# Attention scores as three 64-row products per segment, with two heads in different rows of the array, and the gates' weights copied behind the first layer's operands

## The chip, the cores and the metric

The kernel runs on one core of a Trainium2 chip. It uses TensorE (PE in the profile; its weight loads are PEld), VectorE (DVE), ScalarE (ACT), GpSimd (POOL) and SyncE (SP, which here only issues DMAs). The metric is device time in microseconds (us), the median of the timed runs; less is better.

## The reference

The program is a decoder trunk of two layers on 512 rows of width 1024, in float32. The first mixes rows by gated linear attention, the second by stick-breaking attention over 16 heads of 64; behind each stand a layer norm, an MLP of width 4096 with a squared ReLU, and another layer norm. The change touches the first products of the first layer (a projection of x, of which the last 16 columns feed the forget gates) and the scores of the second layer's attention:

```
proj = x @ w_in
q, k, v, g, a1 = jnp.split(proj, [GLA_QK, 2 * GLA_QK, 2 * GLA_QK + GLA_V, 2 * GLA_QK + 2 * GLA_V], axis=-1)
log_a = jax.nn.log_sigmoid((a1 @ w_a2 + b_a).astype(jnp.float32)) / GATE_TAU
...
def stick_breaking_attention(q, k, v):
    # A[t,s] = sigmoid(z_ts) * prod_{s<j<t} (1 - sigmoid(z_tj)), z = q.k / sqrt(dh)
    for i in range(S // BLOCK_Q):                      # 4 blocks of 128 queries
        kv_len = (i + 1) * BLOCK_Q                     # causal: 128, 256, 384, 512 keys
        z = jnp.einsum('bqhd,bkhd->bhqk', q_blk, k_blk) * scale
        mask = s_idx[None, :] < t_idx[:, None]
        log_1m = jnp.where(mask, jax.nn.log_sigmoid(-z), 0.0)
        rev = lax.cumsum(log_1m, axis=3, reverse=True)
        log_w = jax.nn.log_sigmoid(z) + (rev - log_1m)
        w = jnp.where(mask, jnp.exp(log_w), 0.0)
        outs.append(jnp.einsum('bhqk,bkhd->bqhd', w, v_blk))
```

## The kernel before

**Products in three parts.** A float32 operand is split into a rounded part `hi` (type fp32r, an ACT copy) and the rest `lo` (a DVE subtract); `put` (L97 to L99) does both for a tile in PSUM or SBUF, `split_piece` (L70, L72) for a loaded piece of weights. A product is then three matmuls into one PSUM bank, hi x hi, hi x lo and lo x hi (`mm3`, lines L93, L94, L95). Rounded operands make a product of 512 columns take one pass. Where the operands stay float32, as in the transposes and in L826, it is the slower float32 form.

**PSUM.** There are eight banks of 512 float32 columns, given out in turn by `bank()`. A new tile waits until the last reader of the bank that it gets is done.

**Order.** Work is written in one order, and a scheduler places the instructions of each engine from it; instructions that are passed through `keep_in_program_order` stay in the written order among themselves.

**The start (L430 to L469).** x comes as eight tiles of 128 x 512 (L438, `h`), the first weights as eight pieces (L445, `raw`), alternating on SP's queue. For each step k from 0 to 7, four transposes turn the tile of x (L121), ACT and DVE copy the transposed tile out (`T`, L98 and L99) and split the weights (`hi`, `lo`, the same lines), and the products of the step before follow (L93 to L95, 96 of them in all). Transposes without a use (`warm`, L434 and L453) fill the first microseconds. In step 5 `gate_weights()` is called: it loads the gates' weights `wa_raw` and `a2` by eight small DMAs on SP (L408 to L423), copies `wa` on ACT and DVE (L411, L412), and splits `a2`. The first use of `wa` is the product of L468, behind the 96 products; `a2_hi` follows later.

**Attention (L755 to L880).** Eight pairs of heads, p = 0 to 7; a pair fills 128 partitions, one head in partitions 0 to 63 and the other in 64 to 127. Of a pair:
- `keys()` and `queries()` project 128 columns of keys or queries: 24 products of 512 columns (L93 to L95) into one bank. Out of it the tiles for the scores are made. They hold, for each head, hi and lo stacked over 128 rows: `kh` is the keys' hi in both halves of the rows (an ACT copy, L767, and a POOL copy into the other half, L770), `kl` the keys' lo in the head's own half beside zeros (DVE, L768), `qs` the queries' hi in the own half and lo in the other (ACT, L776; DVE, L777). Each works on the 64 partitions of one head, so each is done twice.
- `weights()` computes the scores in five tiles of one bank each (L790): for each of the segments of 512, 384 + 128, and 256 columns, two products of 128 rows, with `kh` and with `kl`. That is 16 products for the pair. Then DVE adds the mask (L794), ACT takes two sigmoids (`r`, L799; `w`, L800), DVE scans `r` (L802), and POOL (DVE for the last tile) multiplies (L803).
- `turn()` transposes the five tiles `w` (L812, four transposes for a tile) and copies them on ACT to `wt` (L817, eight copies for five tiles). It is a generator, and goes on by one tile each time that it is asked.
- `outputs()` multiplies `wt` with the values (L826): 16 products of 64 output rows, alternating between the heads, each head in its own half of the array's columns.

In the loop, turn p runs `keys` of pair p+2, then `queries` of pair p+2, during whose products the turning of pair p goes on (one tile behind each k of 4, 5, 6 and 7, by the table TAKE, and what is left at the end), then `weights` of pair p+1, then `outputs` of pair p. In p = 6 and 7, where no keys are left to project, the four row tiles of the output projection take their place.

Of the kernel before, what the change touches and what calls it, by code (L numbers as in the profile page):

```python
# [14 lines left out]
P = 128  # L15
S = 512
# [18 lines left out]
def yoco_kernel(ctx: ExitStack, tc: tile.TileContext, x, gla_w_in, gla_w_a2, gla_b_a, gla_norm_g,  # L35
# [369 lines left out]
    def gate_weights():  # L405

        wa_raw = gtp.tile([P, 8, RANK], F32, name="wa_raw")
        nc.sync.dma_start(out=wa_raw, in_=w_in[:, 2 * QK + 2 * D:].rearrange("(a p) c -> p a c", p=P))  # L408
        wa = gtp.tile([P, 8, P], F32R, name="wa")
        nc.gpsimd.memset(wa.bitcast(F32), 0.0)  # L410
        nc.scalar.activation(wa[:, :, 0:RANK], wa_raw, AF.Copy)  # L411
# [12 lines left out]
        return wa, a2_hi, a2_lo  # L424

# [10 lines left out]
    for u in range(2):  # L436
        for t in range(NT):
            nc.sync.dma_start(out=xs[t][:, 512 * u:512 * u + 512],  # L438
                              in_=x2[128 * t:128 * t + 128, 512 * u:512 * u + 512])
            if t % 2 == 0:  # L440
                trio = [wts.tile([P, 1024], dt, tag=tag, bufs=n, name=nm(tag))
                        for tag, dt, n in (("raw", F32, 3), ("hi", F32R, 6), ("lo", F32R, 6))]
            raw, hi, lo = (w[:, 512 * (t % 2):512 * (t % 2) + 512] for w in trio)
            k = 4 * u + t
            nc.sync.dma_start(out=raw, in_=w_in[128 * k:128 * k + 128, 2 * QK:2 * QK + 512])  # L445
            transpose_into(xT, u, t, xs[t][:, 512 * u:512 * u + 512], keep=tc.keep_in_program_order)
            put(hi, lo, raw, keep=tc.keep_in_program_order)
# [290 lines left out]
    kls = [sbp.tile([P, 2, S], F32R, name=f"kl{i}") for i in range(2)]  # L738
    for kl in kls:
        nc.gpsimd.memset(kl[DH:P, 0, :].bitcast(F32), 0.0)  # L740
        nc.gpsimd.memset(kl[0:DH, 1, :].bitcast(F32), 0.0)

    def chain():
        return sbp.tile([P, S], F32, tag="w", bufs=6, name=nm("w"))

# [10 lines left out]
    class Pair:  # L756


        def __init__(self, p):
            self.p = p  # L760

        def keys(self):
            ps = cols(h2T, piece_128(kv_w, P * self.p))
            self.kh = sbp.tile([P, 2, S], F32R, tag="kh", bufs=2, name=nm("kh"))
            self.kl = kls[self.p % 2]
            for a, (own, other) in enumerate(HALVES):
                nc.scalar.activation(self.kh[own, a, :], ps[own, :], AF.Copy)  # L767
                nc.vector.tensor_tensor(self.kl[own, a, :], ps[own, :], self.kh[own, a, :].bitcast(F32),  # L768
                                        op=ALU.subtract)
                nc.gpsimd.tensor_copy(out=self.kh[other, a, :], in_=self.kh[own, a, :])  # L770

        def queries(self, mid=None):
            ps = cols(h2T, piece_128(sb_w_q[0], P * self.p), mid)
            self.qs = sbp.tile([P, 2, S], F32R, tag="qs", bufs=2, name=nm("qs"))
            for a, (own, other) in enumerate(HALVES):
                nc.scalar.activation(self.qs[own, a, :], ps[own, :], AF.Copy, scale=DH ** -0.5)  # L776
                nc.vector.scalar_tensor_tensor(self.qs[other, a, :], ps[own, :], DH ** -0.5,  # L777
                                               self.qs[own, a, :].bitcast(F32), op0=ALU.mult, op1=ALU.subtract)

        def weights(self):  # L780

            self.ws = []
            for kind, segs in ((0, ((0, 3, 0),)), (1, ((0, 2, 0), (0, 0, 384))), (0, ((1, 3, 0),)),
                               (1, ((1, 2, 0), (1, 0, 384))), (2, ((0, 1, 0), (1, 1, 256)))):
                z = bank()
                for a, i, f in segs:
                    q = self.qs[:, a, P * i:P * i + P]
                    n = P * (i + 1)
                    for k, end in ((self.kh, False), (self.kl, True)):
                        nc.tensor.matmul(z[:, f:f + n], lhsT=q, rhs=k[:, a, 0:n], start=not end, stop=end)  # L790

                z4 = z.rearrange("p (b c) -> p b c", c=P)
                last = (z4[:, 3:4, :], z4[:, 2:4, :], z4[:, 1::2, :])[kind]
                nc.vector.tensor_tensor(last, last, low.unsqueeze(1).broadcast_to([P, last.shape[1], P]), op=ALU.add)  # L794
# [137 lines left out]
```

## Time and profile before

| | us |
|---|---|
| median of 3 runs (least, most) | 1143.9 (1143.76, 1144.88) |
| the profiled execution's own time | 1144.64 |
| its span | 1142.7 |
| PE busy | 1115.5 |
| DVE, ACT, POOL busy | 815.2, 554.2, 180.9 |

The span is the time between the first and the last recorded instruction; the profiled execution's own time is 1.9 us longer. In the rows below, L12 is line 12 of the kernel; x4 behind a shape counts instructions that are printed as one row; a bracket at the end of a row is the time that the engine had been idle, and what it waited for. A matmul's busy time holds its way through the array, which overlaps the next one's: the pace of the engine is read from start to start.

### The profile page before, as it was taken

Reading aid. Unit: us, or ns where it says so; the run is one execution under the profiler, and the core shown is the slowest. Engines: PE = TensorE matmul, PEld = TensorE weight load, DVE = VectorE, ACT = ScalarE, POOL = GpSimd, SP = SyncE. Lnnn points to the kernel's source line nnn. Section 1 sums busy time; section 2 is a strip of 40 time slices with the busy share of each in tenths; the row PEclk is TensorE's granted clock in tenths of the full one; section 3 lists DMA queues with packets and bytes.
Section 4 is the critical chain, followed back from the end, with each engine's and each line's share of the span. In section 5 each row is a group of like instructions: output and inputs, shape, how many; then the busy total and the mean of one; then the engine's idle time right before and its main releaser. Section 6 shows DMA issues by size and latency. Waiting matters only on the chain.

```text
span 1142.7 us, 14176 instructions
## 1 busy us (share of the span) xinstructions
PE 1115.5 (98%) x5435; PEld 927.9 (81%) x5435; DVE 815.2 (71%) x992; ACT 554.2 (48%) x823; POOL 180.9 (16%) x217
## 2 busy tenths in 40 slices
PE   7999999999999999999999999999999999999995
PEld 6888888898888888888788877787988888888884
DVE  2678738977757847839946878796767767567578
ACT  2554436553533534536635575654544435336262
POOL 1010123010000100121202435350100000001221
PEclk8999999999999999999999999999999999999998
DMA  7531299492670770886344121211864815706871
GB/s 214 148 111 56 81 267 204 132 295 109 180 207 21 201 203 19 216 189 129 94 128 129 56 75 37 74 38 37 241 202 115 240 51 150 227 28 185 193 120 74
DMA packets 104936, 156.47 MB, mean 137 GB/s; under 512 B 12258, under 2 KB 37218, under 8 KB 104868
## 3 DMA queue, kind: packets, MB, share of 16 engines
q1 hardware_dynamic: 86916, 120.96, 33.1%
q0 software_dynamic: 17952, 34.61, 17.6%
q8 instruction: 42, 0.69, 0.2%
q14 instruction: 26, 0.21, 0.1%
HBM read 153.45 MB, written 2.10 MB: 136 GB/s over the span
## 4 chain that ended last, share of the span: by engine, by line
PE 86%; DVE 8%; ACT 3%; issue 1%; DMA 1%; POOL 0%; SPq 0%; DVEq 0%; ACTq 0%; POOLq 0%
PE ps L336 26%; PE ps L93 18%; PE ps L94 18%; PE ps L95 18%; DVE lo L72 2%; PE ps L826 2%; PE ps L812 1%; ACT wt L817 1%; DVE T L99 1%; DVE h L168 1%; DVE bst L175 1%; ACT hi L70 1%; DVE r L802 1%; DVE h L194 1%; DMA h<-in_x_dram 1%
## 5 line engine op out<-in xcount | busy, mean ns | idle before, releaser
L336 PE MATMUL ps<-hi,T 128*128 128x512 f32 x1008 | 313.2, 390 | 0.0
L93 PE MATMUL ps<-T,hi 128*128 128x512 f32 (+1 forms) x768 | 288.3, 376 | 0.0
L94 PE MATMUL ps<-T,hi 128*128 128x512 f32 (+1 forms) x768 | 285.7, 372 | 0.9 <-DVE T L99 0.8
L95 PE MATMUL ps<-T,lo 128*128 128x512 f32 (+1 forms) x768 | 285.3, 372 | 0.0
L72 DVE TENSOR_TENSOR lo<-raw,hi 128x1024 fp32r<-128x1024 f32 x134 | 164.1, 1228 | 131.9 <-ACT hi L70 131.4
L70 ACT ACTIVATE hi<-raw 128x1024 fp32r<-128x1024 f32 x134 | 142.5, 1065 | 179.8 <-PE ps L336 62.1
L336 PEld LDWEIGHTS ps<-hi,T 128*128 128x128 f32 x1008 | 188.9, 188 | 40.1 <-DVE T L99 0.8
L336 PE MATMUL ps<-lo,T 128*128 128x512 f32 x504 | 196.3, 389 | 0.0
L72 DVE TENSOR_TENSOR lo<-B,hi 128x1024 fp32r<-128x1024 f32 x108 | 130.9, 1223 | 88.5 <-ACT hi L70 88.3
L70 ACT ACTIVATE hi<-B 128x1024 fp32r<-128x1024 f32 x108 | 114.3, 1059 | 150.3 <-PE ps L94 78.7
L95 PEld LDWEIGHTS ps<-T,lo 128*128 128x128 f32 x768 | 144.6, 188 | 25.3
L94 PEld LDWEIGHTS ps<-T,hi 128*128 128x128 f32 x768 | 144.8, 189 | 24.9 <-DVE T L99 1.3
L93 PEld LDWEIGHTS ps<-T,hi 128*128 128x128 f32 x768 | 144.5, 188 | 24.7 <-issue 0.9
L290 POOL DMA_DIRECT2D B<-in_mlp_w_down_dram x52 | 62.4, 1226 | 539.2 <-DMA B<-in_mlp_w_down_dram 464.8
L336 PEld LDWEIGHTS ps<-lo,T 128*128 128x128 f32 x504 | 94.6, 188 | 19.5
L93 PE MATMUL ps<-hi,T 128*128 128x512 f32 x256 | 103.0, 402 | 5.2 <-ACT T L98 5.2
L94 PE MATMUL ps<-lo,T 128*128 128x512 f32 x256 | 100.9, 394 | 0.8 <-DVE lo L72 0.8
L95 PE MATMUL ps<-hi,T 128*128 128x512 f32 x256 | 100.8, 394 | 0.0
L168 DVE TENSOR_TENSOR h<-h,ps 128x512 f32<-128x512 f32 x110 | 74.6, 682 | 5.2 <-PE ps L95 3.6
L803 POOL TENSOR_TENSOR w<-w,r 128x512 f32<-128x512 f32 x32 | 55.0, 1720 | 55.7 <-DVE r L802 38.4
L802 DVE TENSOR_TENSOR_SCAN r<-r,begin 128x512 f32<-128x512 f32 x40 | 61.1, 1559 | 0.2
L93 PEld LDWEIGHTS ps<-hi,T 128*128 128x128 f32 x256 | 48.5, 189 | 15.1 <-ACT T L98 5.4
(173 smaller groups left out, 1203.0 us busy)
## 6 DMA issues: line engine op xcount, KB each, us to landing
raw<-in_mlp_w_up_dram SPq DMA_DIRECT2D x64, 512.0 KB, 5.4
B<-in_mlp_w_down_dram SPq DMA_DIRECT2D x64, 512.0 KB, 5.8
B<-in_mlp_w_down_dram POOLq DMA_DIRECT2D x52, 512.0 KB, 7.9
raw<-in_gla_w_in_dram SPq DMA_DIRECT2D x20, 512.0 KB, 3.7
raw<-in_mlp_w_down_dram SPq DMA_DIRECT2D x16, 512.0 KB, 4.9
raw<-in_kv_w_dram SPq DMA_DIRECT2D x16, 512.0 KB, 3.7
B<-in_gla_w_o_dram POOLq DMA_DIRECT2D x14, 512.0 KB, 9.5
B<-in_gla_w_o_dram SPq DMA_DIRECT2D x8, 512.0 KB, 8.3
```

What stands on the lines that cost most here:

```text
L70: nc.scalar.activation(hi, raw, AF.Copy)
L72: nc.vector.tensor_tensor(lo, raw, hi.bitcast(F32), op=ALU.subtract)
L93: nc.tensor.matmul(ps, lhsT=a[0], rhs=b[0], start=first, stop=False)
L94: nc.tensor.matmul(ps, lhsT=a[0], rhs=b[1], start=False, stop=False)
L95: nc.tensor.matmul(ps, lhsT=a[1], rhs=b[0], start=False, stop=last)
L99: keep(nc.vector.tensor_tensor(lo, ps, hi.bitcast(F32), op=ALU.subtract))
L168: nc.vector.tensor_tensor(h, h, ps, op=op)
L290: nc.gpsimd.dma_start(out=b.rearrange("p (a b) -> p a b", a=2), in_=weights(k, h, j), accum_op=ALU.add)
L336: nc.tensor.matmul(banks[s], lhsT=a(k, s)[x], rhs=b[k][y], start=opens and (k, x, y) == (0, 0, 0), stop=closes and (k, x, y) == (3, 1, 0), ...
L802: nc.vector.tensor_tensor_scan(down, down, begins[kind][:, ::-1], 1.0, op0=ALU.mult, op1=ALU.max)
L803: (nc.vector if kind == 2 else nc.gpsimd).tensor_tensor(w, w, r[:, 1:S + 1], op=ALU.mult)
L826: nc.tensor.matmul(ops[HALVES[a][0], P * j:512], lhsT=vs[hd // 8][:, j, DH * (hd % 8):DH * (hd % 8) + DH], rhs=self.wt[a][:, 512 * j:512 * ...
```

## The change

Three parts.

1. The gates' weights: `gate_weights()` is called behind the loop of the first products instead of in its step 5, and both of its splits go through `put` in the written order.
2. The scores: the tiles of a pair are `kh`, `kl`, `qh`, `ql`, each with both heads over 128 partitions, so each is one instruction (two for the keys, two for the queries). POOL's copies and the zeros beside `kl` are gone. `scores()` makes three products of 64 rows for each segment and head (qh x kh, qh x kl, ql x kh), 24 for a pair, the two heads by turns, each from its own half of the rows and into its own bank: six banks instead of five. The last tile's two segments of 256 lie in two banks, so its mask and sigmoids are done in halves (six adds instead of five, twelve sigmoids instead of ten).
3. The turning: TAKE asks for two tiles behind k = 4, so all five are turned while the queries are projected; in p = 7 the four row tiles take 1, 1, 2 and 1 instead of 0, 1, 2 and 2.

```diff
@@ gate_weights()
-        nc.scalar.activation(wa[:, :, 0:RANK], wa_raw, AF.Copy)
-        nc.vector.tensor_tensor(wa[:, :, 32:32 + RANK], wa_raw, wa[:, :, 0:RANK].bitcast(F32), op=ALU.subtract)
+        put(wa[:, :, 0:RANK], wa[:, :, 32:32 + RANK], wa_raw, keep=tc.keep_in_program_order)
...
-        put(a2_hi, a2_lo, a2)
+        put(a2_hi, a2_lo, a2, keep=tc.keep_in_program_order)
@@ the loop of the first products
-            if k == 5:
-                wa, a2_hi, a2_lo = gate_weights()
...
+    wa, a2_hi, a2_lo = gate_weights()
     for j, kk in todo.pop():
         mm3(pss[j], xT.k(kk, 128 * j, 128), pcs[kk], kk == 0, kk == 7)
@@ class Pair
         def keys(self):
             ps = cols(h2T, piece_128(kv_w, P * self.p))
-            self.kh = sbp.tile([P, 2, S], F32R, tag="kh", bufs=2, name=nm("kh"))
-            self.kl = kls[self.p % 2]
-            for a, (own, other) in enumerate(HALVES):
-                nc.scalar.activation(self.kh[own, a, :], ps[own, :], AF.Copy)
-                nc.vector.tensor_tensor(self.kl[own, a, :], ps[own, :], self.kh[own, a, :].bitcast(F32),
-                                        op=ALU.subtract)
-                nc.gpsimd.tensor_copy(out=self.kh[other, a, :], in_=self.kh[own, a, :])
+            self.k = self.part("kh"), self.part("kl")
+            put(*self.k, ps)
...
-            for a, (own, other) in enumerate(HALVES):
-                nc.scalar.activation(self.qs[own, a, :], ps[own, :], AF.Copy, scale=DH ** -0.5)
-                nc.vector.scalar_tensor_tensor(self.qs[other, a, :], ps[own, :], DH ** -0.5,
-                                               self.qs[own, a, :].bitcast(F32), op0=ALU.mult, op1=ALU.subtract)
+            self.q = qh, ql = self.part("qh"), self.part("ql")
+            nc.scalar.activation(qh, ps, AF.Copy, scale=DH ** -0.5)
+            nc.vector.scalar_tensor_tensor(ql, ps, DH ** -0.5, qh.bitcast(F32), op0=ALU.mult, op1=ALU.subtract)
+
+        def scores(self):
+            zs = [bank() for _ in range(6)]
+            for i, b, f in ((3, 0, 0), (2, 2, 0), (0, 2, 384), (1, 4, 0)):
+                n = P * (i + 1)
+                for x, y in ((0, 0), (0, 1), (1, 0)):
+                    for a, (own, _) in enumerate(HALVES):
+                        at = slice(f + 256 * a * (i == 1), f + n + 256 * a * (i == 1))
+                        nc.tensor.matmul(zs[b + a][:, at], lhsT=self.q[x][own, P * i:P * i + P],
+                                         rhs=self.k[y][own, 0:n], start=(x + y == 0), stop=(x == 1),
+                                         skip_group_check=True)
+            return zs
@@ weights()
-                    for k, end in ((self.kh, False), (self.kl, True)):
-                        nc.tensor.matmul(z[:, f:f + n], lhsT=q, rhs=k[:, a, 0:n], start=not end, stop=end)
...
-                nc.scalar.activation(rb, z, AF.Sigmoid, scale=-1.0)
-                nc.scalar.activation(w, z, AF.Sigmoid)
+                for at, z in views:
+                    nc.scalar.activation(rb[:, at], z, AF.Sigmoid, scale=-1.0)
+                    nc.scalar.activation(w[:, at], z, AF.Sigmoid)
@@ the loop over the pairs
-    TAKE = {4: 1, 5: 1, 6: 1, 7: 1}
+    TAKE = {4: 2, 5: 1, 6: 1, 7: 1}
...
-            for _ in made:
-                pass
...
-                for _ in range((0, 1, 2, 2)[t]):
+                for _ in range(((0, 1, 2, 2), (1, 1, 2, 1))[n][t]):
                     next(made, None)
```

Two places of the new order. On ACT, at the start of the program, this is the difference (`T_101` are transposed tiles of x, `hi_121` the first split weights, `wa` the gates'):

```order
 L126 ACT_TABLE_LOAD
 L98 ACTIVATE T_101<-ps_124 128x4x128
 L98 ACTIVATE hi_121<-raw_120 128x512
-L411 ACTIVATE wa<-wa_raw 128x8x16
 L98 ACTIVATE T_101<-ps_145 128x4x128
 L98 ACTIVATE hi_121<-raw_120 128x512
```

The copy of `wa` stood ahead of the second transposed tile. It now stands behind the last operands of this stage:

```order
-L98 ACTIVATE T_103<-ps_303 128x4x128
-L98 ACTIVATE hi_280<-raw_279 128x512
+L98 ACTIVATE T_103<-ps_284 128x4x128
+L98 ACTIVATE hi_261<-raw_260 128x512
+L98 ACTIVATE wa<-wa_raw 128x8x16
+L98 ACTIVATE a_hi<-a_314 128x512
 L70 ACTIVATE hi_387<-raw_385 128x1024
```

(The first four rows are the last operands of the stage, the same ones under other buffer numbers.)

On SP the eight small loads of the gates' weights stood ahead of the last two tiles of x (`h_95`, `h_96`) and the last two pieces of weights; before:

```order
L445 DMA raw_211<-in_gla_w_in_dram 128x512
L408 DMA wa_raw<-in_gla_w_in_dram 128x8x16
L417 DMA a_262<-in_gla_w_a_dram 16x512
L418 DMA a_262<-in_gla_b_a_dram 1x512
...
L423 DMA normg<-in_gla_norm_g_dram 128x256
L438 DMA h_95<-in_x_dram 128x512
L445 DMA raw_279<-in_gla_w_in_dram 128x512
L438 DMA h_96<-in_x_dram 128x512
```

And now:

```order
L444 DMA raw_211<-in_gla_w_in_dram 128x512
L437 DMA h_95<-in_x_dram 128x512
L437 DMA h_96<-in_x_dram 128x512
L408 DMA wa_raw<-in_gla_w_in_dram 128x8x16
L416 DMA a_314<-in_gla_w_a_dram 16x512
...
L444 DMA raw_260<-in_gla_w_in_dram 128x512 x2
L417 DMA a_314<-in_gla_b_a_dram 1x512
```

Both tiles of x moved ahead of all the gates' loads; the last two pieces of weights stand behind five of those eight.

On PE, in the loop over the pairs, the end of a projection of queries (L93 to L95, with the transposes of the `w` tiles between), the scores, and the first of the outputs (`wt` is the turned weights, `T_4595` the values); before:

```order
L95 MATMUL ps_5345<-T_4179,lo_5343 128x512
L812 MATMUL ps_5403<-ident,w_5284 128x128 x4
L790 MATMUL ps_5410<-kh_5151,qs_5217 128x512
L790 MATMUL ps_5410<-kl_4589,qs_5217 128x512
L790 MATMUL ps_5421<-kh_5151,qs_5217 128x384
```

And now:

```order
L95 MATMUL ps_5348<-T_4179,lo_5346 128x512
L778 MATMUL ps_5412<-kh_5149,qh_5219 128x512
L778 MATMUL ps_5413<-kh_5149,qh_5219 128x512
L778 MATMUL ps_5412<-kl_5150,qh_5219 128x512
L778 MATMUL ps_5413<-kl_5150,qh_5219 128x512
L778 MATMUL ps_5412<-kh_5149,ql_5220 128x512
L778 MATMUL ps_5413<-kh_5149,ql_5220 128x512
```

The last transposes no longer stand between the projection and the scores, and the products of the two heads alternate between two banks. The two forms of L790 before have 128 rows of contraction each, the three forms of L778 have 64.

More of the change, by code (lines that the diff above doesn't have):

```diff
@@ L736, in yoco_kernel @@
     begins = (begin[:, 0:512], begin[:, 128:640], begin[:, 256:768])
[L738 to L741, printed above, removed]
     def chain():
@@ L760, in __init__, with part @@
             self.p = p
+        def part(self, tag):
+            return sbp.tile([P, S], F32R, tag=tag, bufs=2, name=nm(tag))
         def keys(self):
             ps = cols(h2T, piece_128(kv_w, P * self.p))
-            self.kh = sbp.tile([P, 2, S], F32R, tag="kh", bufs=2, name=nm("kh"))
-            self.kl = kls[self.p % 2]
-            for a, (own, other) in enumerate(HALVES):
-                nc.scalar.activation(self.kh[own, a, :], ps[own, :], AF.Copy)
-                nc.vector.tensor_tensor(self.kl[own, a, :], ps[own, :], self.kh[own, a, :].bitcast(F32),
-                                        op=ALU.subtract)
-                nc.gpsimd.tensor_copy(out=self.kh[other, a, :], in_=self.kh[own, a, :])
+            self.k = self.part("kh"), self.part("kl")
+            put(*self.k, ps)
@@ L772, in queries @@
         def queries(self, mid=None):
             ps = cols(h2T, piece_128(sb_w_q[0], P * self.p), mid)
-            self.qs = sbp.tile([P, 2, S], F32R, tag="qs", bufs=2, name=nm("qs"))
-            for a, (own, other) in enumerate(HALVES):
-                nc.scalar.activation(self.qs[own, a, :], ps[own, :], AF.Copy, scale=DH ** -0.5)
-                nc.vector.scalar_tensor_tensor(self.qs[other, a, :], ps[own, :], DH ** -0.5,
-                                               self.qs[own, a, :].bitcast(F32), op0=ALU.mult, op1=ALU.subtract)
+            self.q = qh, ql = self.part("qh"), self.part("ql")
@@ L780, in weights @@
         def weights(self):
             self.ws = []
[L783 to L788, printed above, removed]
-                    for k, end in ((self.kh, False), (self.kl, True)):
[L790 to L794, printed above, removed]
+            zs = self.scores()
@@ new lines, in weights @@
+            for kind, segs, banks in ((0, ((0, 3, 0),), (0,)), (0, ((1, 3, 0),), (1,)), (1, ((0, 2, 0), (0, 0, 384)), (2,)),
+                                      (1, ((1, 2, 0), (1, 0, 384)), (3,)), (2, ((0, 1, 0), (1, 1, 256)), (4, 5))):
+                n = S // len(banks)
+                views = [(slice(n * i, n * i + n), zs[b][:, n * i:n * i + n]) for i, b in enumerate(banks)]
+                for _, z in views:
+                    z4 = z.rearrange("p (b c) -> p b c", c=P)
+                    last = z4[:, (slice(3, 4), slice(2, 4), slice(1, 2))[kind], :]
+                    nc.vector.tensor_tensor(last, last, low.unsqueeze(1).broadcast_to([P, last.shape[1], P]),
+                                            op=ALU.add)
```

## The prediction

> **What bounds the kernel now.** I read the page's busy times first, then the chain that ended last:
>
> ```profile
> span 1142.7 us, 14176 instructions
> PE 1115.5 (98%) x5435; PEld 927.9 (81%) x5435; DVE 815.2 (71%) x992; ACT 554.2 (48%) x823; POOL 180.9 (16%) x217
> PE 86%; DVE 8%; ACT 3%; issue 1%; DMA 1%; POOL 0%; SPq 0%; DVEq 0%; ACTq 0%; POOLq 0%
> ```
>
> PE is the bound almost everywhere. A change can gain in only two ways: less streaming on PE, or less of PE's idle time, some 27 us in all. ACT, DVE and POOL count only where PE waits for them. So I read PE's timeline at both places of the change, start to start.
>
> **The start.** PE's, ACT's and SP's timelines, and two windows (columns: length; busy time of PE, PEld, DVE, ACT and POOL; granted clock; DMA share; GB/s):
>
> ```profile
> 5.94 0.60 PE L121 MATMUL ps<-ident,h 128*128 128x128 f32 x4
> 8.74 0.66 PE L121 MATMUL ps<-ident,h 128*128 128x128 f32 x4 [1.07 <-DMA h<-in_x_dram]
> 14.61 0.80 PE L93 MATMUL ps<-hi,T 128*128 128x512 f32 x1 [5.21 <-ACT T L98]
> 18.19 0.63 PE L95 MATMUL ps<-hi,T 128*128 128x512 f32 x1
> 18.62 0.76 PE L121 MATMUL ps<-ident,h 128*128 128x128 f32 x4
> 19.14 0.47 PE L93 MATMUL ps<-hi,T 128*128 128x512 f32 x1
> 40.17 0.40 PE L95 MATMUL ps<-hi,T 128*128 128x512 f32 x1
> 40.40 0.39 PE L468 MATMUL ps<-T,wa 128*128 128x512 f32 x1
> ...
> 13.76 0.31 ACT L411 ACTIVATE wa<-wa_raw 128x128 fp32r<-128x128 f32 x1 [7.99 <-DMA wa_raw<-in_gla_w_in_dram]
> 13.98 0.58 ACT L98 ACTIVATE T<-ps 128x512 fp32r<-128x512 f32 x1
> ...
> 8.71 0.38 SPq L408 DMA_DIRECT2D wa_raw<-in_gla_w_in_dram  x1
> ...
> 12.00:13.00 1.00, 0.00 (x0) 0.00 (x0) 0.00 (x0) 0.00 (x0) 0.00 (x0) 0.56 0.36 77
> 15.00:20.00 5.00, 5.00 (x17) 3.87 (x17) 2.08 (x4) 1.67 (x5) 0.00 (x0) 0.61 0.70 230
> ```
>
> ACT runs in order. Its third copy is that of `wa`, which waits 7.99 us for a load that SP issues only at 8.71, and the copy of the second transposed tile (`T`, 13.98) stands behind it. PE had transposed that tile at 5.94 and the next one at 8.74; the products on the first of these start at 14.61. The nine products then run at a granted clock of 0.61, .43 from start to start (18.19 to 18.62), where a product at full clock takes .23 (40.17 to 40.40).
>
> Without `wa` in the queue, ACT copies the second tile soon after 5.94, and splits its weights as they land. The nine products then follow the transposes of 8.74 in PE's order. Behind transposes a product started .52 later at the slow clock (18.62 to 19.14), .28 at full clock if all of it scales (.52 x .23 / .43); I take the middle, 9.13. That is **5.48** earlier. PE's idle stretch shrinks from 5.21 us to about one, like the 1.07 before 8.74, so the clock should stay up and the nine products run at .23: 9 x .20 = **1.8** more, and **.1** for the transposes behind them. The 87 products after those follow without a gap, so the stage's end moves from 40.40 to about 33.0: **-7.4**.
>
> What could be late next: the data. By 12 us DMA had fallen to a share of 0.36, with only the small loads left, so the operands of steps 0 to 5 are there by then; of these, step 3's tile is asked for at about 11.2 and step 4's at 15. The last two steps' operands are asked for at 21 to 24. SP now issues their tiles of x where the gates' loads began, at 8.7 and .7 later; their weights, behind five small loads, at about 12 to 13. Loads of this kind land, by their group (KB, median us from issue to landing):
>
> ```profile
> raw<-in_gla_w_in_dram SPq DMA_DIRECT2D x8, 256.0 KB, 5.3
> ```
>
> That is 14 to 18 us: in time, and the gates' own loads have until 33. Behind the stage come pieces of weights that PE asks for 7 us earlier than before; I price that at nothing and keep 4 us, half the gain, as the other end.
>
> **Attention, a pair in the steady part.** PE's timeline of pair 1 and pair 0, and of pair 6; then the chain in order of time, and the wait in the list of waits (us in total, times, longest):
>
> ```profile
> 657.64 0.48 PE L790 MATMUL ps<-kh,qs 128*128 128x512 f32 x1
> ...
> 660.16 0.28 PE L790 MATMUL ps<-kl,qs 128*128 128x256 f32 x1
> 661.30 2.64 PE L826 MATMUL ps<-wt,T 128*64 128x512 f32 x16 [0.86 <-ACT wt L817]
> 663.87 0.50 PE L93 MATMUL ps<-T,hi 128*128 128x512 f32 x1
> ...
> 638.90 0.48 PE L790 MATMUL ps<-kh,qs 128*128 128x512 f32 x1
> 644.43 0.50 PE L93 MATMUL ps<-T,hi 128*128 128x512 f32 x1
> ...
> 754.81 0.48 PE L790 MATMUL ps<-kh,qs 128*128 128x512 f32 x1
> 757.33 0.28 PE L790 MATMUL ps<-kl,qs 128*128 128x256 f32 x1
> 757.53 2.38 PE L826 MATMUL ps<-wt,T 128*64 128x512 f32 x16
> 759.84 0.50 PE L93 MATMUL ps<-hi,T 128*128 128x512 f32 x1
> ...
> 659.60 0.94 ACT hi L70
> 660.54 0.44 ACT qs L776
> 660.98 0.28 ACT wt L817
> ...
> PE ps L826 <- ACT wt L817: 5.5, 6, 1.1
> ```
>
> From the first score to the next projection: 6.23 us in the steady pairs (663.87 - 657.64; I count p = 1 to 5, since the wait occurs six times, the sixth in p = 7), 5.53 in p = 0, 5.03 in p = 6. The steady ones wait: the last turned tile is copied on ACT behind a split of weights and a copy of queries, and the outputs start 1.14 us behind the last score (660.16 to 661.30). In p = 6, without that wait, the step to the outputs' form takes .20, of which .12 is the last score; so changing the form costs **.09** (.20 less the .12 that such a score takes, rows below).
>
> The paces of the scores, in the first scores, which stand alone:
>
> ```profile
> 617.86 0.39 PE L790 MATMUL ps<-kh,qs 128*128 128x512 f32 x1
> 618.09 0.39 PE L790 MATMUL ps<-kl,qs 128*128 128x512 f32 x1
> 618.31 0.33 PE L790 MATMUL ps<-kh,qs 128*128 128x384 f32 x1
> 618.48 0.34 PE L790 MATMUL ps<-kl,qs 128*128 128x384 f32 x1
> ...
> 620.28 0.28 PE L790 MATMUL ps<-kl,qs 128*128 128x256 f32 x1
> 620.40 0.40 PE L93 MATMUL ps<-T,hi 128*128 128x512 f32 x1
> ```
>
> .23 for 512 columns, .17 for 384, .12 for 256, and by the same pace (.45 ns a column) .06 for 128; there the weights' load, itself 128 columns, bounds it, and I take .11, the time of 256 columns, as an estimate. The stage takes 2.54. Now there are three products for each segment and head instead of two. If the two heads run at once, the stage costs three passes of one head: 3 x (.23 + .17 + .12 + .11) = 1.89, and .09 for its form: **1.98**. If each takes its turn, it is twice 1.89, **3.8**; below nothing is excluded, since no product gets shorter than its columns. No row of before has two products of 64 rows; the nearest is L826, where the heads use different halves of the columns. Its group (least, median, most ns), and the first .10 us of p = 6's, of L826 alone:
>
> ```profile
> L826 PE MATMUL ps<-wt,T x128: 272/432/644, 641.9 to 776.8; 128*64 128x512 f32 x32, 128*64 128x384 f32 x32, 128*64 128x256 f32 x32, 128*64 128x128 f32 x32
> 757.50:757.60 0.10, 0.07 (x2) 0.07 (x4) 1.00 0.94 369
> ```
>
> Two products and four loads start within .07 us. A product's time holds about .16 beside its pace (.39 against .23 above), so 16 of .43 would take 16 x .27 = 4.3 one behind the other; they take 2.31 (757.53 to 759.84). So different parts of the array do work at once, and I take 1.98.
>
> The Trainium skill (TensorE: Matmul & The Clock Gate, Part 3: Packing small matmuls) says that products in different row groups run together, but not for nothing: four of 32 rows gave 3.07 times the speed. If two lost in that proportion, the stage would be 3.8 / 1.54, some 2.5 instead of 1.9, an estimate from that page: 4 to 5 us more in all. No run here shows it.
>
> Then the outputs: 2.31, as in p = 6, if nothing has to be waited for. In steady pairs they take 2.57 (661.30 to 663.87), since the two heads' copies come one behind the other and the second starts late. With two tiles turned behind k = 4, the last transposes stand ahead of the last three products, so the last copy can be done while the scores run. So the new stretch is 1.98 + .09 + 2.31 = **4.38**. Sum: 5 x (6.23 - 4.38) = 9.25; p = 0, 1.15; p = 6, .65; the first scores alone, 2.54 - 1.98, less .09 for the way back, = .47; p = 7, the late start of one head, 2.57 - 2.31, about .25. 9.25 + 1.15 + .65 + .47 + .25 = 11.8: **-11.8**.
>
> What ACT and DVE now do besides, by a window of the steady part:
>
> ```profile
> 670.00:690.00 20.00, 19.12 (x104) 15.52 (x103) 16.63 (x20) 13.00 (x27) 9.48 (x12) 1.00 0.16 54
> ```
>
> DVE is busy 16.63 of 20 us and POOL 9.48. The copies over 128 partitions take two DVE and two ACT instructions off a pair, and POOL's copies go; one add and two half sigmoids come. A pair's turn takes 19.4 now (754.81 - 657.64 over five) and 17.6 then; DVE's load of 16.1 in it falls by about 1.2 to 14.9, so it still fits, and PE's streaming hides it. Six banks at once instead of five one behind another make the scores wait for those who read these banks before: ACT's copies to `wt` and DVE's split of the keys. No row of before shows these waits. They cost nothing if the readers are done, and at the other end the .86 to 1.1 a pair of the wait that was removed; I take nothing, as in p = 6.
>
> **Sum.** 1144.64 - 7.4 - 11.8 = 1125.4 against the profiled execution, which is .7 above the median of the runs; I predict 1125.
>
> **Rivals.**
> (a) *Loads or the array's sharing bound the short segments.* 24 loads of .11 a pair, if they don't overlap, are 2.6 a stage instead of 1.98: 8 x .65 = 5.2, so 1130; if they overlap but none hides behind its own head's products, twelve by .11 stand in each head's way, 3 x (.58 + .44) = 3.1, so 1134. For it: PEld is at 81%, and the short segments' products are no longer than their loads. Against: in L826's window four loads start with two products.
> (b) *No overlap, the change doesn't do what it says*: 3.8 a stage, 8 x 1.89 = 15 more: 1140. Still faster, by the start and the waits. For it: no row of 64-row products. Against: L826.
> (c) *A wait takes the place of the one removed*, in one of the two parts: the .86 to 1.1 before the outputs, or at the banks, comes back in five or six pairs, or half the start's gain goes to late data: 4 to 5 us, so 1129. For it: ACT's copies are what PE waited for, and six banks make more waits on them. Against: a tile more is turned before.
> (d) *Slower*: 64-row products stream like L826's form, one pass of ten blocks in 2.31: three passes are 6.9 a stage instead of 1.98, 8 x 4.9 = 39 more: 1164. It decides from 4.4 a stage on (1.98 + 19.2 / 8). For it: L826's products are the only split ones here. Against: their operands are float32, those of the scores fp32r, as in L790.
>
> The Trainium skill (TensorEngine Tiling (Array Packing), Key Properties) says that changing the form drains the array, which speaks against mixing a third form in. The rows agree (.09 to .10 a change), and the sum holds them.
>
> **Chances.** Forecast .70; (a) .13; (b) .09; (c) .05; (d) .03. Forecast's own range 1121 to 1128: the low end if changes of form and the short segments' loads cost nothing (8 x .5), the high end if (a) holds by half. 8 in 10 takes in (a) and (c): 1121 to 1135. A measurement can tell about 0.2%, 2.3 us, from no change: faster .95, same .02 (between b and d), slower .03.
>
> **What would show it.** In the profile after: `wa` behind the last `hi` on ACT, no 5.21 wait in front of the second products, and the gates' first product at about 33. In the pairs: L778's rows in twos, their starts nearly equal, the stage 1.9 to 2.0 (3.8 under b, 2.6 under a); no wait of L829 on `wt`; first score to next projection 4.4. Wrong if L778's starts are spaced evenly, or PE's idle time shows a new releaser, DVE's `ql` or `kl` above all.

## The result, and the profile after

| | us |
|---|---|
| before, median (least, most) | 1144.36 (1143.76, 1144.88), 4 runs |
| changed, median (least, most) | 1127.17 (1126.48, 1130.78), 4 runs |
| ratio to before, 95% interval | 0.9856 [0.9834, 0.9878] |
| span of the profiled execution, before and changed | 1142.7 and 1124.4 |

The change takes off 17.2 us by the medians and 18.3 by the spans. The page of the changed kernel begins with the span, PE's busy time, and later the shares of the chain that ended last:

```profile
span 1124.4 us, 14299 instructions
PE 1108.1 (99%) x5499; PEld 917.8 (82%) x5499; DVE 806.1 (72%) x984; ACT 547.5 (49%) x823; POOL 166.4 (15%) x197
PE 91%; DVE 7%; issue 1%; ACT 1%; POOL 0%; DVEq 0%; POOLq 0%; ACTq 0%
```

PE's busy time falls by 7.4 us and its idle time (span less busy) from 27.2 to 16.3. ACT's share of the chain goes from 3% to 1%, and DMA's is gone. So over half of the gain is waiting that no longer happens. Here is the start on PE's timeline:

```profile
7.70 0.66 PE L121 MATMUL ps<-ident,h 128*128 128x128 f32 x4
8.11 0.48 PE L93 MATMUL ps<-hi,T 128*128 128x512 f32 x1
10.04 0.40 PE L95 MATMUL ps<-hi,T 128*128 128x512 f32 x1
10.28 0.60 PE L121 MATMUL ps<-ident,h 128*128 128x128 f32 x4
31.90 0.39 PE L466 MATMUL ps<-T,wa 128*128 128x512 f32 x1
```

And the window in which the granted clock had been 0.61 (the same columns as in the prediction, the clock the third from the end):

```profile
15.00:20.00 5.00, 5.00 (x25) 4.13 (x25) 1.29 (x2) 0.89 (x2) 0.00 (x0) 1.00 0.82 200
```

The wait of 5.21 is gone, the nine products run at .23 each, and the gates' first product comes at 31.90 instead of 40.40. About 1 us of that is chance: the tile of x that is turned just ahead of these nine products was there at 7.70 instead of 8.74.

A steady turn of the pairs, on the same timeline: the projection's last product, the first and the last scores, the outputs, and the first product of the next projection. Below it, the first scores of all and the last outputs with the product behind them:

```profile
647.89 0.40 PE L95 MATMUL ps<-T,lo 128*128 128x512 f32 x1
648.21 0.50 PE L778 MATMUL ps<-kh,qh 64*128 64x512 f32 x2
648.55 0.39 PE L778 MATMUL ps<-kl,qh 64*128 64x512 f32 x2
648.78 0.40 PE L778 MATMUL ps<-kh,ql 64*128 64x512 f32 x2
...
650.12 0.28 PE L778 MATMUL ps<-kh,ql 64*128 64x256 f32 x2
650.33 2.37 PE L829 MATMUL ps<-wt,T 128*64 128x512 f32 x16
652.63 0.50 PE L93 MATMUL ps<-T,hi 128*128 128x512 f32 x1
...
609.48 0.50 PE L778 MATMUL ps<-kh,qh 64*128 64x512 f32 x2
756.10 2.64 PE L829 MATMUL ps<-wt,T 128*64 128x512 f32 x16 [0.98 <-ACT wt L820]
758.67 0.50 PE L93 MATMUL ps<-hi,T 128*128 128x512 f32 x1
```

The last outputs and the product behind them in the kernel before:

```profile
774.41 2.65 PE L826 MATMUL ps<-wt,T 128*64 128x512 f32 x16 [1.09 <-ACT wt L817]
776.99 0.50 PE L93 MATMUL ps<-hi,T 128*128 128x512 f32 x1
```

A window at the first scores, of L778 alone (columns: length; busy time of PE and PEld; granted clock; DMA share; GB/s):

```profile
648.20:648.25 0.05, 0.04 (x2) 0.04 (x2) 1.00 1.28 358
```

Each row of the scores holds two products (x2), one of each head, and the rows follow at the pace that one product had before: .23 for 512 columns (648.55 to 648.78). The window shows that the two start together: both, with their loads, are under way within .05 us. From the first score to the next projection it is 4.42 us instead of 6.23, with no wait before the outputs; only p = 7 still waits. Attention, from its first score to the first product behind its last outputs, takes 758.67 - 609.48 = 149.19, before 776.99 - 617.86 = 159.13: **9.94 less**. That stretch is called attention's below, and is taken from the same two rows of each kernel's profile.

### The profile page after: what moved, and what is told of

It is laid out like the page before. It is cut to its first block, busy times and chain, and to the rows that moved or that the text cites. A ratio compares the mean times of both kernels' runs of the same rounds, so it can differ in the third digit from the quotient of the medians.

```text
span 1124.4 us, 14299 instructions
## 1 busy us (share of the span) xinstructions
PE 1108.1 (99%) x5499; PEld 917.8 (82%) x5499; DVE 806.1 (72%) x984; ACT 547.5 (49%) x823; POOL 166.4 (15%) x197
## 4 chain that ended last, share of the span: by engine, by line
PE 91%; DVE 7%; issue 1%; ACT 1%; POOL 0%; DVEq 0%; POOLq 0%; ACTq 0%
PE ps L336 27%; PE ps L93 19%; PE ps L94 19%; PE ps L95 19%; DVE lo L72 2%; PE ps L829 2%; PE ps L815 2%; PE ps L778 2%; DVE T L99 1%; DVE h L168 1%; DVE bst L175 1%; DVE h L194 1%; DVE h L217 0%; POOL rs L184 0%; PE ps L557 0%
## 5 line engine op out<-in xcount | busy, mean ns | idle before, releaser
L93 PE MATMUL ps<-T,hi 128*128 128x512 f32 (+1 forms) x768 | 288.4, 376 | 0.0
L95 PE MATMUL ps<-T,lo 128*128 128x512 f32 (+1 forms) x768 | 285.4, 372 | 0.0
L336 PEld LDWEIGHTS ps<-hi,T 128*128 128x128 f32 x1008 | 189.0, 188 | 40.1 <-DVE T L99 0.8
L95 PEld LDWEIGHTS ps<-T,lo 128*128 128x128 f32 x768 | 144.7, 188 | 25.2
L93 PEld LDWEIGHTS ps<-T,hi 128*128 128x128 f32 x768 | 144.5, 188 | 24.8 <-issue 0.9
L336 PEld LDWEIGHTS ps<-lo,T 128*128 128x128 f32 x504 | 94.6, 188 | 19.5
L93 PE MATMUL ps<-hi,T 128*128 128x512 f32 x256 | 102.3, 400 | 0.0
L95 PE MATMUL ps<-hi,T 128*128 128x512 f32 x256 | 100.1, 391 | 0.0
L805 DVE TENSOR_TENSOR_SCAN r<-r,begin 128x512 f32<-128x512 f32 x40 | 66.2, 1659 | 2.4 <-ACT r L802 2.2
L94 PEld LDWEIGHTS ps<-lo,T 128*128 128x128 f32 x256 | 48.2, 188 | 10.9 <-DVE lo L72 1.4
```

The lines of the kernel that those rows point to most:

```text
L93: nc.tensor.matmul(ps, lhsT=a[0], rhs=b[0], start=first, stop=False)
L94: nc.tensor.matmul(ps, lhsT=a[0], rhs=b[1], start=False, stop=False)
L95: nc.tensor.matmul(ps, lhsT=a[1], rhs=b[0], start=False, stop=last)
L336: nc.tensor.matmul(banks[s], lhsT=a(k, s)[x], rhs=b[k][y], start=opens and (k, x, y) == (0, 0, 0), stop=closes and (k, x, y) == (3, 1, 0), ...
```

## The experiments

### The start: which of the two edits does it

**g_both**, the whole of the gates' part in the kernel before; **g_keep**, only the written order (`put` with `keep` for both splits, the call still in step 5); **g_move**, only the moved call.

```diff
 (g_keep)
-        nc.scalar.activation(wa[:, :, 0:RANK], wa_raw, AF.Copy)
-        nc.vector.tensor_tensor(wa[:, :, 32:32 + RANK], wa_raw, wa[:, :, 0:RANK].bitcast(F32), op=ALU.subtract)
+        put(wa[:, :, 0:RANK], wa[:, :, 32:32 + RANK], wa_raw, keep=tc.keep_in_program_order)
-        put(a2_hi, a2_lo, a2)
+        put(a2_hi, a2_lo, a2, keep=tc.keep_in_program_order)
 (g_move)
-            if k == 5:
-                wa, a2_hi, a2_lo = gate_weights()
+    wa, a2_hi, a2_lo = gate_weights()
     for j, kk in todo.pop():
```

> The kernel before with the gates' part alone (both splits through put in the written order, the call behind the loop). Theory: the start's gain stands by itself and is all of it a matter of ACT's order, so the gates' first product comes at 32 to 33 us as in the changed kernel and the time falls by 7.5 to 8.5 us, to about 1136. Rival: the earlier end of the start is eaten later, where the next pieces of weights are late: less than 6 us.

> The kernel before with the written order alone: both splits through put, the call left in step 5 and its loads on SP ahead of the last two steps' operands. Theory (ACT's order is the cause, SP's is not): almost the whole gain, -7 to -8.5 us, the last two steps' operands landing at 18 to 21 us just in time. Rival (SP's order matters): the wait moves to the operands of steps 6 and 7 and a third or more of the gain is missing, -5 us or less.

> The kernel before with the call moved alone, without the written order: the copy of wa then stands on ACT one step later, behind the second operands and ahead of the third. Theory: PE does the second step's nine products at about 8 us at full clock and then waits for the third step's until wa has landed, at about 14 us; the start ends 3 to 4 us later than with both edits: -3 to -5 us. Rival (the load's place on SP is what counts): -7 us or more.

| | median us (before beside it: 1144.46) | ratio, 95% interval | gates' first product at |
|---|---|---|---|
| g_both | 1136.61 | 0.9938 [0.9915, 0.9961] | 32.25 |
| g_keep | 1137.23 | 0.9935 [0.9920, 0.9950] | 32.36 |
| g_move | 1143.53 | 0.9995 [0.9985, 1.0005] | 39.29 |

The written order alone brings 7.2 of the 7.9 us. Where the loads stand on SP, and in which step the call is written, hardly matters. g_move brought less than either theory gave. Its profile shows why, first on ACT's timeline:

```profile
14.35 0.31 ACT L411 ACTIVATE wa<-wa_raw 128x128 fp32r<-128x128 f32 x1 [5.46 <-DMA wa_raw<-in_gla_w_in_dram]
```

On PE's:

```profile
11.00 0.39 PE L95 MATMUL ps<-hi,T 128*128 128x512 f32 x1
11.23 0.60 PE L121 MATMUL ps<-ident,h 128*128 128x128 f32 x4
15.20 0.79 PE L93 MATMUL ps<-hi,T 128*128 128x512 f32 x1 [3.37 <-ACT T L98]
```

And in a window behind that wait:

```profile
16.00:18.00 2.00, 2.00 (x6) 1.60 (x6) 2.00 (x4) 1.19 (x3) 0.00 (x0) 0.50 0.17 53
```

The copy of `wa` stands one step later and blocks the third step's operands. The second step's nine products are done at 11.2, but the next wait is 3.37 us, and behind it the granted clock is 0.50, as it was in the kernel before. Now it is the third step's fifteen products, all but the last two, that run at that clock, instead of the second step's nine. What the nine gained is paid back.

The start itself varies from one execution to the next: the gates' first product comes at 38.90 to 40.73 in four profiles with the start as before (before, att, b_newtake, b_keyfirst) and at 31.90 to 32.69 in those with both edits. So some 7.5 us is the gain, and 40.40 to 31.90 was a favourable pair.

### Attention alone

**att**, the changed kernel with the gates' part undone.

```diff
+            if k == 5:
+                wa, a2_hi, a2_lo = gate_weights()
...
-    wa, a2_hi, a2_lo = gate_weights()
```

(and the two splits as before.)

> The changed kernel with the gates' part undone: scores in 64-row products, copies over 128 partitions, the new TAKE. Theory: the two parts don't touch each other; attention brings 9.9 us as in the changed kernel's marks, so about 1134.5, and the sum of this and the gates' part alone is the whole within a microsecond. Rival: they share a cause (the start's earlier end shifts loads that attention waits for) and the sum misses by over 2 us.

1134.64 us, 9.8 less than 1144.46 beside it, ratio 0.9910 [0.9895, 0.9925]; attention's stretch is 149.19, that of the changed kernel. With g_both's 7.9 the sum is 17.7, where the whole is 17.2: the parts don't touch each other.

### The order of the turning: TAKE

**a_oldtake**, the changed kernel with the old TAKE; **b_newtake**, the kernel before with the new one.

```diff
 (a_oldtake; b_newtake is the reverse, in the kernel before)
-    TAKE = {4: 2, 5: 1, 6: 1, 7: 1}
+    TAKE = {4: 1, 5: 1, 6: 1, 7: 1}
...
+            for _ in made:
+                pass
...
-                for _ in range(((0, 1, 2, 2), (1, 1, 2, 1))[n][t]):
+                for _ in range((0, 1, 2, 2)[t]):
```

> The changed kernel with the old TAKE (one tile behind each k of 4 to 7, the fifth behind the projection; 0, 1, 2, 2 in p = 7). Theory: the early turning is what removed the wait before the outputs; with a shorter score stage in front of it (2.1 instead of 2.5) the wait comes back in p = 1 to 5 at 1.1 to 1.5 us each and the two heads' outputs start apart again (.26): +6 to +9 us over the changed kernel. Rival: the lighter copies on ACT removed it, and the old TAKE costs under 2 us.

> The kernel before with the new TAKE alone, its scores as they were. Theory: the stretch from first score to next projection falls from 6.23 to 5.03 in p = 1 to 5 as it is in p = 6 of before, -5 to -6.5 us in all, so more than half of attention's gain is the order and the rest the shorter stage. Rival: the wait goes to another place (the banks, or POOL's copies of the keys) and less than 2 us is gained.

Beside 1144.32 of before: a_oldtake 1127.37, ratio 0.9843 [0.9827, 0.9860]; b_newtake 1143.86, ratio 0.9998 [0.9985, 1.0010]. Attention's stretch is 149.35 and 158.96. Both theories of mine fell: the order of the turning costs nothing when undone and brings nothing alone. b_newtake on ACT's timeline:

```profile
690.55 0.58 ACT L767 ACTIVATE kh<-ps 64x512 fp32r<-64x512 f32 x1
695.49 0.59 ACT L767 ACTIVATE kh<-ps 64x512 fp32r<-64x512 f32 x1 [4.36 <-DVE kl L768]
696.11 2.75 ACT L817 ACTIVATE wt<-ps 128x512 f32<-128x512 f32 x8
```

And on PE's, at the second tile of the scores:

```profile
696.76 0.44 PE L790 MATMUL ps<-kh,qs 128*128 128x384 f32 x1 [1.10 <-ACT wt L817]
```

All five tiles are turned early on PE, yet all eight copies to `wt` start only at 696.11, behind ACT's second copy of the keys. PE now waits for them earlier, at a bank of the scores. The wait moved; it did not go. What holds ACT is the copy that waits 4.36 us for DVE. The kernel before has the same wait, in the turn that the prediction read; on its ACT's timeline:

```profile
652.18 0.59 ACT L767 ACTIVATE kh<-ps 64x512 fp32r<-64x512 f32 x1
656.78 0.59 ACT L767 ACTIVATE kh<-ps 64x512 fp32r<-64x512 f32 x1 [4.01 <-DVE kl L768]
657.40 2.19 ACT L817 ACTIVATE wt<-ps 128x512 f32<-128x512 f32 x6
```

And on its DVE's:

```profile
652.94 1.31 DVE L803 TENSOR_TENSOR w<-w,r 128x512 f32<-128x512 f32 x1
654.17 0.68 DVE L99 TENSOR_TENSOR T<-ps,T 128x512 fp32r<-128x512 f32 x1
654.77 1.38 DVE L72 TENSOR_TENSOR lo<-raw,hi 128x1024 fp32r<-128x1024 f32 x1
656.08 0.68 DVE L768 TENSOR_TENSOR kl<-ps,kh 64x512 fp32r<-64x512 f32 x1
```

`keys()` writes copy, subtract, copy, subtract, and the second copy carries a wait on DVE for the first subtract, though the two work on different halves of the tiles. DVE, in its order, gets to that only at 656.08. Until it is done, ACT stands still with the copies to `wt` behind it.

### The keys' two copies

**b_keyfirst**, the kernel before with both copies of the keys ahead of the two subtracts, which takes the wait out of the program; **a_splitcopy**, the changed kernel with the keys split head by head again.

```diff
 (b_keyfirst)
             for a, (own, other) in enumerate(HALVES):
                 nc.scalar.activation(self.kh[own, a, :], ps[own, :], AF.Copy)
+            for a, (own, other) in enumerate(HALVES):
                 nc.vector.tensor_tensor(self.kl[own, a, :], ps[own, :], self.kh[own, a, :].bitcast(F32),
 (a_splitcopy)
-            put(*self.k, ps)
+            for own, _ in HALVES:
+                put(self.k[0][own, :], self.k[1][own, :], ps[own, :])
```

> The kernel before with one edit in keys(): ACT's copies of both heads are written ahead of DVE's two subtracts, instead of copy, subtract, copy, subtract. Nothing else differs, and ACT's second copy then no longer waits for DVE. Theory: that wait (4.0 us on ACT, with the copies to wt queued behind it) is what held PE before the outputs, so the outputs follow the scores in .21 us in p = 1 to 5 and their 2.57 become 2.30: -5 to -7 us. Rival: the length of the copies or POOL's part holds the turned tiles back, and less than 2 us is gained.

> The changed kernel with the keys split head by head again (copy, subtract, copy, subtract over 64 partitions each), all else as changed, the new TAKE too. Theory: ACT's second copy waits for DVE again with the copies to wt behind it, and PE waits at the banks of the scores, as with the new TAKE alone: +4 to +7 us over the changed kernel. Rival: with POOL's copies gone and DVE lighter it waits too briefly to matter: under 2 us.

Beside 1144.33 of before: b_keyfirst 1138.52, ratio 0.9951 [0.9935, 0.9968], attention's stretch 152.66, 6.47 less than before. Its five runs lie from 1137.03 to 1141.80, and the profiled one is the longest: at 233 us, ahead of attention and where the edit changes nothing, PE waits 2.35 us for DVE (0.21 in before). So the stretch says more here than the time. On PE's timeline the wait is gone, although the last tile is still turned behind the projection:

```profile
660.67 0.60 PE L813 MATMUL ps<-ident,w 128*128 128x128 f32 x4
661.02 0.48 PE L791 MATMUL ps<-kh,qs 128*128 128x512 f32 x1
663.55 0.28 PE L791 MATMUL ps<-kl,qs 128*128 128x256 f32 x1
663.76 2.38 PE L827 MATMUL ps<-wt,T 128*64 128x512 f32 x16
666.07 0.50 PE L93 MATMUL ps<-T,hi 128*128 128x512 f32 x1
```

5.05 from first score to next projection instead of 6.23, and .21 from the last score to the outputs. a_splitcopy is the reverse: 1137.38, ratio 0.9935 [0.9921, 0.9948], attention's stretch 159.44, 10.25 longer than in the changed kernel and more than expected. ACT's second copy waits for DVE again, on ACT's timeline:

```profile
687.76 0.59 ACT L98 ACTIVATE kh<-ps 64x512 fp32r<-64x512 f32 x1 [3.72 <-DVE kl L99]
```

And PE, on its own, waits for the copies to `wt` at the scores:

```profile
689.03 0.49 PE L779 MATMUL ps<-kh,qh 64*128 64x512 f32 x1 [0.89 <-ACT wt L821]
```

Behind the outputs it waits once more, in each of p = 1 to 5, for DVE's part of the queries:

```profile
694.10 0.50 PE L93 MATMUL ps<-T,hi 128*128 128x512 f32 x1 [0.54 <-DVE ql L768]
```

One line in either direction: the interleaving of copy and subtract was the cause of the wait. In p = 2 to 5 the scores, up to the outputs, take 3.54 instead of 2.12, and the outputs, up to the next projection, 2.91 instead of 2.30, of which the wait for `ql` is .54. That makes some 2.0 a turn, more than the wait cost in the kernel before.

### What is left for the 64-row form

**g_keyfirst**, the kernel before with the gates' part and with b_keyfirst's edit: both waits gone, the scores in their old form.

```diff
-            if k == 5:
-                wa, a2_hi, a2_lo = gate_weights()
+    wa, a2_hi, a2_lo = gate_weights()
...
+            for a, (own, other) in enumerate(HALVES):
                 nc.vector.tensor_tensor(self.kl[own, a, :], ps[own, :], self.kh[own, a, :].bitcast(F32),
```

> The kernel before with the gates' part and ACT's two copies of the keys ahead of DVE's subtracts, the scores in their old form of 16 products of 128 rows and the old TAKE. Theory: the two waits are gone, 7.5 us at the start and 6.5 in attention, so about 1130.5; what is then missing to the changed kernel, 3 to 4 us (.42 a score stage, eight stages, and the last wait), is all that the 64-row form itself brings. Rival: the 64-row form brings more than its stage shows (lighter DVE and POOL elsewhere): 1133 or more here.

1130.19 us (1129.76 to 1130.45) beside 1145.82 of before, ratio 0.9865 [0.9849, 0.9882]; attention's stretch 152.67. The changed kernel's stretch is 3.48 less, and that is what the new scores bring, with all that is left of the change: one copy and one subtract for the queries, no copies on POOL, the new TAKE. The times tell it less well: the changed kernel's median is 3.0 less, but set against the before beside each it is 1.6 (17.2 and 15.6 off), and the two intervals overlap.

### The order of the heads

**a_headwise**, for each segment three products of one head, then three of the other; **a_head12**, all twelve of one head, then all of the other.

```diff
 (a_headwise)
-                for x, y in ((0, 0), (0, 1), (1, 0)):
-                    for a, (own, _) in enumerate(HALVES):
+                for a, (own, _) in enumerate(HALVES):
+                    for x, y in ((0, 0), (0, 1), (1, 0)):
 (a_head12)
+            for a, (own, _) in enumerate(HALVES):
+                for i, b, f in ((3, 0, 0), (2, 2, 0), (0, 2, 384), (1, 4, 0)):
```

> The changed kernel with the heads not by turns: for each segment the three products of one head, then the three of the other. Theory: products start in their order, and one starts beside another only if it stands right behind it and is in other rows, so only the borders overlap; a segment takes four or five slots instead of three and the stage goes from 2.1 to about 2.7: +4 to +6 us. Rival A (no overlap without turns at all): 3.8 a stage, +14 us. Rival B (PE takes products out of order): no change.

> The changed kernel with all twelve products of one head written ahead of the twelve of the other. Theory A (each half of the rows takes its own next product, however far behind in the order): still no change, within 2 us. Theory B (PE looks only some products ahead): the stage goes from 2.1 toward 4 us, +5 to +15 us.

a_headwise: 1127.41, ratio 0.9843 [0.9823, 0.9862], no change. The second head's first product is the fourth in the program, and starts .010 us behind the first and ahead of the second; in the timeline the two share a row (x2), and the pace is as before. a_head12: 1139.34, ratio 0.9952 [0.9938, 0.9966], 12.2 us more than the changed kernel; the stage, to the outputs, takes 3.63 (652.40 to 656.03) instead of 2.12, and eight times the difference is 12.1. A row of PE's timeline in a_headwise:

```profile
649.16 0.51 PE L778 MATMUL ps<-kh,qh 64*128 64x512 f32 x2
```

And rows of a_head12's:

```profile
652.40 0.50 PE L778 MATMUL ps<-kh,qh 64*128 64x512 f32 x1
653.79 0.27 PE L778 MATMUL ps<-kl,qh 64*128 64x128 f32 x1
653.90 0.27 PE L778 MATMUL ps<-kh,ql 64*128 64x128 f32 x1
653.91 0.50 PE L778 MATMUL ps<-kh,qh 64*128 64x512 f32 x2
656.03 2.37 PE L829 MATMUL ps<-wt,T 128*64 128x512 f32 x16
```

The second head's first product, the thirteenth in the program, starts beside the ninth (653.90; the x2 of 653.91 takes in the tenth, which starts .10 later). So it gets ahead of the tenth, eleventh and twelfth, three products of the other rows, and not of more. (In six of the eight stages a copy on ACT ends some .013 us before it starts. In the first and the last none does, and it starts beside the ninth all the same, so this isn't what it waits for.)

### The last wait

**a_p7early**, the changed kernel with the last tile of p = 7 turned behind the third row tile.

```diff
-                for _ in range(((0, 1, 2, 2), (1, 1, 2, 1))[n][t]):
+                for _ in range(((0, 1, 2, 2), (1, 2, 2, 0))[n][t]):
```

> The changed kernel with the four row tiles of p = 7 taking 1, 2, 2, 0 tiles instead of 1, 1, 2, 1. Theory: the last copies to wt then stand ahead of the two splits of weights on ACT, the wait of .98 us before the last outputs goes and the two heads start together: about -1.2 us in the marks, at the edge of what the times can tell. Rival: the last w is not ready by then, and PE waits in front of the transposes instead: 0.

1126.10 us (1125.49 to 1126.47, five runs), ratio to before 0.9835 [0.9822, 0.9849]. Attention's stretch is 147.97, 1.22 less than in the changed kernel, and PE's timeline has no wait there:

```profile
755.81 0.39 PE L95 MATMUL ps<-hi,T 128*128 128x512 f32 x1
756.13 2.15 PE L829 MATMUL ps<-wt,T 128*64 128x512 f32 x12
```

It beats both kernels by its median, though its interval overlaps the changed kernel's; the stretch is what shows it.

## Why the prediction was right, and where it was wrong

The time, 1127.17, lies 2.2 us above the 1125 forecast and inside the range. One part was right with its reason. The other came out near with a wrong reason for the larger half of it, and that is luck: the change held what removes the wait, but for the sake of the scores' form.

- **The start, -7.4: right.** 7.2 and 7.9 by g_keep and g_both. The cause is as told: ACT's copy of `wa` stood ahead of operands. g_move adds that the half clock behind the wait is a large part of its price. The rival of late data didn't occur; operands and pieces were in time even in g_keep, where the gates' loads stayed ahead on SP.
- **The wait before the outputs: gone as forecast, but not for the reason given.** The step that failed is "With two tiles turned behind k = 4, the last transposes stand ahead of the last three products, so the last copy can be done while the scores run." a_oldtake and b_newtake show that the order of the turning does nothing here. The copies over 128 partitions do it, of which the prediction counted only the lighter load ("it still fits, and PE's streaming hides it"): one copy instead of copy, subtract, copy, subtract has no place at which ACT waits for DVE. The chain of waits had named only what stood between the wait's end and the outputs (a split and a copy of queries). The 4 us at which ACT stood idle ahead of these lay one step further back, on ACT's own timeline, behind the bracket "<-DVE kl".
- **The 64-row products: right.** Starts .003 us apart, no loss by sharing: 1.91 from the first start to the last, to which the last product's .12 is added and .11 for the first one's change of form taken off, is 1.92 where 1.89 was forecast. Rivals (a), (b) and (d) asked for stages of 2.6 or 3.1, 3.8 and 6.9, and are excluded. Rival (c) did not come either: from the first score to the last output PE waits only once, the .98 in p = 7. The estimate by the Trainium skill (TensorE: Matmul & The Clock Gate, Part 3: Packing small matmuls), 2.5 for the streaming, doesn't hold for two groups of 64 rows: two heads run as fast as one.
- **The size, -11.8: too much by 1.9.** The term that was mis-sized is the change of form. The prediction booked .09 into the scores and .09 out of them. The rows show .10 before the first score (647.89 to 648.21, some .33 instead of .23), .11 in it (648.21 to 648.55, .34), and .09 behind the last. Besides, the slower product behind the last transposes, .08, was the first score before, so it was inside the 6.23, and now stands in the projection. A turn went from 19.43 ((754.81 - 657.64) / 5) to 17.79, -1.64 where -1.85 was forecast. Over the eight stages that is 1.7. The rest, .17, is p = 7, where the wait of .98 and the heads' late start both stayed, because the last copies to `wt` still stand behind two splits of weights on ACT (a_p7early).

By cause, then: some 7.5 us for the copy of `wa` at the start, 6.5 for the copies of the keys, about 3.5 by the stretch (1.6 to 3.0 by the times) for the scores' form and what goes with it, nothing for TAKE.

## What to carry to other kernels

Follow a wait back on the timeline of the engine that is waited for, until that engine is busy and not itself waiting: the cause is there, and moving work behind it moves the wait and no more. Where an engine runs in order, copy and subtract of two halves are best written copy, copy, subtract, subtract, or once over all partitions; and a copy that waits for a late load must be kept behind what is needed now. Two products of 64 rows cost one, as long as each has its partner within a few products in the program (three apart was near enough here, twelve was not); the price is the change of form, some .3 us each time that the array is used so.

## What was not expected of the hardware

- Products that use different halves of the rows need not stand side by side in the program: with three of one head ahead of three of the other they still start .010 us apart (.003 by turns), while with twelve ahead the partner starts beside the ninth in each of the eight stages. So the look-ahead is bounded; three products passed, about four with its own, is what this order shows, and orders between the two were not tried.
- An idle stretch of 1.07 us (before, at 8.74) left the granted clock at 1.00. Behind one of 3.37 (g_move) it was 0.50 for about the next 6 us of work, and behind that of 5.21 (before) for about 4.
